# A two-layer decoder trunk on one core: weight parts of large expert slots taken earlier, a third tile loaded ahead of a loop, small steps of a norm on ScalarE

## The chip, the cores and the metric

One NeuronCore of a Trainium2 chip runs the whole program. Time is device microseconds (us) of one execution; a comparison takes the median of several. Lower is better.

## What is computed

Two layers over 1024 tokens of width 1024, in float32. Layer 0 mixes tokens with a gated DeltaNet beside an S5 state-space model, layer 1 with dilated sliding-window attention. After each mixer comes a hierarchical mixture of experts, and after both a post-norm residual:

```
h = layer_norm(alpha * h + mixer(h))
# per token: best of 4 groups, best 2 of its 8 experts; 32 experts in all
y = gate1 * expert1(h) + gate2 * expert2(h)
expert(x) = (silu(x @ w_gate) * (x @ w_up)) @ w_down      # 1024 -> 512 -> 1024
h = layer_norm(alpha * h + y)       # rsqrt(var + 1e-5), scale, shift
```

The weights of the experts are 6 MB each, 192 MB a layer, and all of them are read in each layer.

## The kernel before

**Slots.** In each layer `moe` runs 32 slots, one an expert. Experts are sorted by how many tokens chose them: the first 16 slots are large (up to 128 tokens), the last 16 are small (up to 64 tokens). The order is three large slots, then rounds of two small and two large ones (S S L L), and at the end S S L S S with large slot 15 between small ones. A round is 24 weight tiles.

**Weights.** An expert's weights come in six tiles of 1 MB (`raw_weights`, L457), all through SP's queue into 17 buffers. Tiles 0 to 3 hold gate and up, tiles 4 and 5 hold down. Load number n waits until load n-3 has landed, so that three are under way; the issue of a load thus marks the landing of the one three before it. A small slot multiplies the raw tile in plain float32 (`small`, L589 and L605). A large slot uses split products: `weights` cuts each tile into halves, ScalarE makes a rounded copy `whi` of each half (L488), VectorE makes the rest `wlo` = raw - `whi` (L490), and TensorE adds three products, hi-hi, lo-hi and hi-lo (L529, L530 for gate and up, L547 for down). The pairs `whi`, `wlo` are the "parts"; there are five buffers for parts, each of one half.

**Order within `moe`.** Each slot is a generator in four pieces: gather and transposition of its rows; halves k = 0 to 3 (tiles 0, 1); halves k = 4 to 7 (tiles 2, 3), the activation `hdn`, its transposition `ph` and split `hh`, `hl`; the down product `po` or `pos` (tiles 4, 5), its copy `ot` or `ots` out of PSUM and a scatter by POOL to `yd`. In program order the first piece of the next slot comes before the third of this one, and the next slot's second piece before this one's fourth. So between halves k = 3 and k = 4 of a large slot that follows a small one stands the small one's down product with its copy `ots` (L618); `ots` is put behind the last `whi` that was traced. Between `hh` of a large slot and its down product stand halves k = 0 to 3 of the next. The order of each engine's instructions is fixed when the program is built, from the program's order and modelled durations.

**The last two slots.** Slots S7 and S15 write no rows to `yd`; their outputs stay in SBUF (`held`), and `combine` adds them by a product with a selection matrix (`hot`). S15 takes all its loads in one go; the last five loads of a layer wait for buffers.

**After the slots.** `tail` and `head` load the first tiles (128 tokens each) of `combine` behind the last weight load: `HEADS` says how many, 1 in layer 0 and 2 in layer 1, with the residual row `ca` and the two expert rows `cyh`. For these VectorE adds the gated rows (L820, L822). Then comes a loop for overflowing experts, which runs no time here (384 weight loads, two times 192), with a point where all engines and the loads under way meet (L747). `scatter_held` then writes the held rows to `yd`, and the other tiles' rows `cy` are read behind it.

**`combine` in layer 1.** Tiles 0 to 3 are summed on TensorE: the residual times the identity or alpha (`al`, L861), plus for t >= 2 two gated rows (`cdg`, L867), plus for t < 2 the held rows (L864). ScalarE copies the sum out with its total (L870), VectorE makes the mean (L881). For tiles 4 to 7 VectorE adds alpha times the residual itself (L872). Then ScalarE squares (L882) while VectorE does (a - mean) * g (L883). `end` of the tile before follows: variance plus eps on VectorE (L887), root on ScalarE (L212), a reciprocal with one Newton step on VectorE (L213 to L216), and the last product and sum (L889). The order on VectorE and ScalarE is by hand: norm(t), then end(t-1). Layer 0's `combine` is alike, with the sums on VectorE and the next layer's value projection (L1078) on TensorE between.

Of the kernel before, what the change touches and what calls it, by code (L numbers as in the profile page):

```python
# [10 lines left out]
F32 = mybir.dt.float32  # L11
# [3 lines left out]
AF = mybir.ActivationFunctionType  # L15
OP = mybir.AluOpType
# [3 lines left out]
D = 1024  # L20
S = 1024
NT = 8
KT = 8
NE = 32
ALPHA = 4.0 ** 0.25
LN_EPS = 1e-5
# [7 lines left out]
LARGE = 16  # L34
# [2 lines left out]
BLOCKS = 24  # L37

PAUSE = (12, 13)

HEADS = (1, 2)

# [115 lines left out]
class Trunk:  # L158
# [48 lines left out]

    def rsqrt(self, v, w):

        nc = self.nc  # L210
        s, r, q, n, o = (w[:, i:i + 1] for i in range(5))
        nc.scalar.activation(s, v, AF.Sqrt)  # L212
        nc.vector.reciprocal(r, s)  # L213
        nc.vector.scalar_tensor_tensor(q, r, v, r, op0=OP.mult, op1=OP.mult)  # L214
        nc.vector.tensor_scalar(n, q, -0.5, 1.5, op0=OP.mult, op1=OP.add)  # L215
        nc.vector.tensor_mul(o, r, n)  # L216
# [288 lines left out]
                                     self.ident)  # L505
        return px.rearrange("p (k t) -> p k t", k=4)

    def large(self, hd, yd, xg, gi, si, wsrc, wk, ps):


        nc = self.nc
        self.hold.setdefault("g", self.gather(hd, xg, gi))
        xh = wk.tile([128, KT, 128], F32R, name="xh", tag="xh")
        xl = wk.tile([128, KT, 128], F32R, name="xl", tag="xl")
        for a in range(2):
            s = self.split(self.transposed(xg, a, ps), xh[:, 4 * a:4 * a + 4], xl[:, 4 * a:4 * a + 4])
            self.hold.setdefault("x", s)
        yield
        pg = ps.tile([128, 512], F32, name="pg", tag="pg")
        pu = ps.tile([128, 512], F32, name="pu", tag="pu")  # L520
        for k in range(KT):
            if k == KT // 2:
                yield
            if k % 2 == 0:
                W = self.weights(wsrc(k // 2))
            hi, lo = W[k % 2]
            for i, (x, w) in enumerate(((xh, hi), (xh, lo), (xl, hi))):
                s, z = k == 0 and i == 0, k == KT - 1 and i == 2
                nc.tensor.matmul(pg, x[:, k], w[:, 0:512], start=s, stop=z)  # L529
                nc.tensor.matmul(pu, x[:, k], w[:, 512:1024], start=s, stop=z)  # L530
        hdn = wk.tile([128, 512], F32, name="hdn", tag="hdn", bufs=1)
        nc.scalar.activation(hdn, pg, AF.Silu)  # L532
        nc.vector.tensor_mul(hdn, pu, hdn)
        ph = ps.tile([128, 512], F32, name="ph", tag="m")
        for f in range(4):
            nc.tensor.transpose(ph[:, f * 128:(f + 1) * 128], hdn[:, f * 128:(f + 1) * 128], self.ident)
        hh = wk.tile([128, 4, 128], F32R, name="hh", tag="hh", bufs=1)
        hl = wk.tile([128, 4, 128], F32R, name="hl", tag="hl", bufs=1)
        self.split(ph.rearrange("p (k t) -> p k t", k=4), hh, hl)
        yield  # L540
        W = [w for q in (4, 5) for w in self.weights(wsrc(q))]
        po = [ps.tile([128, 512], F32, name=f"po{a}", tag="po") for a in range(2)]
        for f in range(4):
            hi, lo = W[f]
            for i, (x, w) in enumerate(((hh, hi), (hh, lo), (hl, hi))):
                for a in range(2):
                    nc.tensor.matmul(po[a], x[:, f], w[:, a * 512:(a + 1) * 512],  # L547
                                     start=(f == 0 and i == 0), stop=(f == 3 and i == 2))
        ot = wk.tile([128, D], F32, name="ot", tag="ot", bufs=1)
        nc.scalar.activation(ot[:, 0:512], po[0], AF.Copy)  # L550
        nc.vector.tensor_copy(ot[:, 512:1024], po[1])
        yield nc.gpsimd.indirect_dma_start(  # L552
            out=yd, out_offset=bass.IndirectOffsetOnAxis(ap=si, axis=0),
            in_=ot, in_offset=None, bounds_check=2 * S - 1, oob_is_err=False)
# [68 lines left out]
    def moe(self, l, hd, yd, first, small, order, place, ov, over, gate, hp, xp, wk, ps, tail):  # L623

        nc, tc = self.nc, self.tc
# [3 lines left out]
        xg = xp.tile([128, D], F32, name="xg")  # L629
# [3 lines left out]
        def enter(s):  # L633
            if s < FIXED:
                def src(q):
                    return wm[l, s, q]
            else:
                reg = []

                def src(q):  # L640
                    if not reg:
                        reg.append(nc.sync.value_load(order[0:1, s:s + 1], min_val=0, max_val=NE - 1))
                    return wmv[ds(reg[0] * 6 + q, 1)].rearrange("a p n -> p (a n)")
            if s < LARGE:
                return self.large(hd, yd, xg, first[:, 1, s:s + 1], first[:, 0, s:s + 1], src, wk, ps)
            j = s - LARGE
            g = SMALL + j % (SMALL // 2)
            return self.small(hd, yd, xg, small[:, g:g + 1], small[:, j:j + 1], src, X,
                              {SMALL // 2 - 1: 0, SMALL - 1: 1}.get(j), wk, ps)


        seq, larges = [*range(FIXED)], list(range(FIXED, LARGE))
        for j in range(SMALL // 2):
            seq += [LARGE + j, LARGE + j + SMALL // 2] + larges[2 * j:2 * j + 2]
        scat = []
        self.ends = [(None, None), None]
        run = enter(seq[0])
# [4 lines left out]
        for i in range(NE):  # L662
# [6 lines left out]
            st = next(run)  # L669
# [154 lines left out]
    def combine(self, l, hd, yd, gate, rows, hot, diag, wk, ps, nx, done):  # L824
# [2 lines left out]

        nc = self.nc
        E = self.held["E"]
        H = len(hot)  # L830
        halves = [slice(c * 512, (c + 1) * 512) for c in range(2)]
        g, b = (wk.tile([128, D], F32, name=n, bufs=1) for n in ("fg", "fb"))
        first = self.bcast_rows(g, self.I["lnfg"][l], D)
        self.bcast_rows(b, self.I["lnfb"][l], D)
        Y, A, ST = {}, dict(enumerate(rows)), {}

        def load(t):
            Y[t] = wk.tile([128, 2, D], F32, name="cy", tag="cy", bufs=NT if l else 3)
            if t >= H:
                A[t] = wk.tile([128, D], F32, name="ca", tag="ca", bufs=NT - H if l else 2)  # L840
                r = self.row_tile(t, hd, A[t], False)
                if l and t > H + 1:
                    self.behind(r, self.loaded)
                self.loaded = self.y_tile(t, yd, Y[t])

# [7 lines left out]
        def norm(t):  # L853
            a, st, y = A[t], ST[t], Y[t]
            if l:
                al, dg = diag
                pe = t < 4
                p = ps.tile([128, D], F32, name="cp", tag="cp", bufs=4)
                for h in halves:
                    if pe:  # L860
                        nc.tensor.matmul(p[:, h], self.ident if t < H else al, a[:, h], start=True, stop=False)  # L861
                for i, h in enumerate(halves):
                    if t < H:
                        nc.tensor.matmul(p[:, h], hot[t][i], E[i], start=False, stop=True)  # L864
                    else:
                        for k in range(2):
                            nc.tensor.matmul(p[:, h], dg[:, t - H, k], y[:, k, h],  # L867
                                             start=(k == 0 and not pe), stop=(k == 1))
                if pe:
                    nc.scalar.activation(a, p, AF.Copy, accum_out=st[:, 0:1])  # L870
                else:
# [1 line left out]
            elif t < H:  # L873
# [4 lines left out]
                    nc.vector.scalar_tensor_tensor(a[:, h], p, 1.0, a[:, h], op0=OP.mult, op1=OP.add,  # L878
                                                   accum_out=st[:, o:o + 1])
                nc.vector.tensor_tensor(st[:, 0:1], st[:, 0:1], st[:, 9:10], op=OP.add)  # L880
            nc.vector.tensor_scalar(st[:, 1:2], st[:, 0:1], -1.0 / D, None, op0=OP.mult)  # L881
            nc.scalar.activation(y[:, 0], a, AF.Square, bias=st[:, 1:2], accum_out=st[:, 2:3])  # L882
            nc.vector.scalar_tensor_tensor(y[:, 1], a, st[:, 1:2], g, op0=OP.add, op1=OP.mult)  # L883

        def end(t):
            a, st, y = A[t], ST[t], Y[t]
            nc.vector.tensor_scalar(st[:, 3:4], st[:, 2:3], 1.0 / D, LN_EPS, op0=OP.mult, op1=OP.add)  # L887
            self.rsqrt(st[:, 3:4], st[:, 4:9])
            nc.vector.scalar_tensor_tensor(a, y[:, 1], st[:, 8:9], b, op0=OP.mult, op1=OP.add)  # L889

        with self.tc.manual_schedule(engines={mybir.EngineType.DVE, mybir.EngineType.Activation}):
# [1194 lines left out]
    def run(self):  # L2086
        nc, I = self.nc, self.I
        with self.pool("c") as p:
# [19 lines left out]
            for l in range(2):  # L2108
# [25 lines left out]
                with self.pool(f"mx{l}", side="right") as xp, self.pool(f"rawb{l}", RAWB, side="right") as rawb, \  # L2134
# [7 lines left out]
                    nx = {}  # L2142

                    def head():
                        for t in range(H):
                            self.row_tile(t, hd, nx["rows"][t], True)
                            self.y_tile(t, yd, nx["ys"][t])
                            e = self.gated(t, nx["rows"][t], nx["ys"][t], gate)
                        return e

                    def tail():
# [9 lines left out]
                            op = hp  # L2161
                        else:
                            vp = op = nx["vp"] = alloc("cr")
                            nx["ys"] = [vp.tile([128, 2, D], F32, name=f"cyh{t}") for t in range(H)]
                            al = vp.tile([128, 128], F32, name="al")
                            nc.vector.tensor_scalar(al, self.ident, ALPHA, None, op0=OP.mult)
                            dg = vp.tile([128, NT - H, 2, 128], F32, name="cdg")
                            for u in range(H, NT):
                                for k in range(2):
                                    nc.vector.tensor_scalar(dg[:, u - H, k], self.ident, gate[:, u, k:k + 1], None,  # L2170
                                                            op0=OP.mult)
                            nx["diag"] = al, dg
                        nx["rows"] = [vp.tile([128, D], F32, name=f"ca{t}") for t in range(H)]
                        nx["hot"] = [self.held_rows(t, [op.tile([128, 128], F32, name=f"hot{l}{t}{e}")
                                                        for e in range(2)]) for t in range(H)]
                        with self.tc.issue_after(self.flight[-1]):
                            if l == 0:
                                self.value_loads(nx["V"], range(1), None)
# [97 lines left out]
```

## Time and profile before

| what | value |
|---|---|
| median of 3 runs | 2457.79 us (2455.66 to 2460.64) |
| the profiled execution's own time | 2459.88 us |
| its span in the profile | 2458.1 us |
| TensorE busy | 92% of the span |
| VectorE, ScalarE busy | 60%, 46% |
| DMA moved | 561.5 MB, mean 228 GB/s |
| mean granted TensorE clock | 0.969 |

PE is TensorE's matmuls, PEld its weight loads, DVE VectorE, ACT ScalarE, POOL GpSimd, SP the engine that issues loads. A wait in the profile is idle time of an engine, put down to what ended it. The expert stages run from about 650 to 1200 us and from 1860 to 2403 us; in what follows a place is one slot's wait.

### The profile page before, as it was taken

What the parts mean: (1) busy time and instruction counts of PE and PEld (TensorE: products, weight loads), DVE (VectorE), ACT (ScalarE), POOL (GpSimd) and SP (SyncE); (2) the same over time, 40 slices, a digit from 0 to 9 for tenths busy, and PEclk for the clock granted to TensorE, in tenths of its full rate; (3) what the DMA queues carried; (4) which work ended last, traced back from release to release, by engine and by line L of the source; (5) the groups of instructions that cost most, each with busy time, mean ns of one, the idle gap of its engine ahead of it and who ended that gap; (6) DMA issues with size and microseconds to landing.
All of it is one profiled execution on the core that took longest, in us unless ns stands there. A gap on an engine that the chain in (4) does not pass through costs nothing. (4 is left out here: it accounts for less than half of the span.)

```text
span 2458.1 us, 34057 instructions
## 1 busy us (share of the span) xinstructions
PE 2258.3 (92%) x11948; PEld 1625.6 (66%) x11948; DVE 1484.9 (60%) x3025; ACT 1141.1 (46%) x1871; POOL 443.9 (18%) x548
## 2 busy tenths in 40 slices
PE   7999999889699999999699999998997999999986
PEld 5888899778555555554377888887875555555542
DVE  7565646557864555554473777778578545555536
ACT  5435454442453544443333666667225534444423
POOL 1545434100114111100001111113001321111100
PEclk9999999899899999999899999999998999999998
DMA  4222222354599999997741000012837999999977
GB/s 166 61 66 42 66 63 72 109 215 158 198 403 373 412 407 410 401 401 309 290 156 49 33 29 33 29 39 85 297 110 288 363 411 405 406 407 406 400 302 269
DMA packets 181728, 561.50 MB, mean 228 GB/s; under 512 B 61570, under 2 KB 98818, under 8 KB 131888
## 3 DMA queue, kind: packets, MB, share of 16 engines
q1 hardware_dynamic: 166000, 525.03, 56.5%
q0 software_dynamic: 15552, 34.25, 3.6%
q8 instruction: 96, 1.57, 0.3%
q14 instruction: 80, 0.66, 0.1%
HBM read 518.76 MB, written 56.43 MB: 234 GB/s over the span
## 5 line engine op out<-in xcount | busy, mean ns | idle before, releaser
L490 DVE TENSOR_TENSOR wlo<-wraw,whi 128x1024 fp32r<-128x1024 f32 x384 | 451.1, 1219 | 144.3 <-ACT whi L488 124.6
L488 ACT ACTIVATE whi<-wraw 128x1024 fp32r<-128x1024 f32 x384 | 383.5, 1053 | 71.9 <-PE pu L530 49.5
L589 PE MATMUL pgs<-wraw,xs 128*64 128x512 f32 x1024 | 241.2, 602 | 1.3 <-ACT hdn L532 0.9
L589 PEld LDWEIGHTS pgs<-wraw,xs 128*64 128x64 f32 x1024 | 68.4, 137 | 129.0 <-issue 117.7
L173 PE MATMUL pj<-xTh,phi 128*128 128x512 f32 x320 | 131.5, 415 | 13.2 <-ACT xTh L446 13.2
L529 PE MATMUL pg<-whi,xh 128*128 128x512 f32 x256 | 108.1, 422 | 28.4 <-ACT whi L488 22.8
L173 PE MATMUL pj<-xTh,plo 128*128 128x512 f32 x320 | 132.2, 414 | 0.0
L173 PE MATMUL pj<-xTl,phi 128*128 128x512 f32 x320 | 130.7, 409 | 0.0
L605 PE MATMUL pos<-wraw,hs 128*64 128x512 f32 x512 | 121.4, 609 | 5.5 <-ACT hdns L592 3.3
L1217 POOL TENSOR_TENSOR plo<-praw,phi 128x256 fp32r<-128x256 f32 x64 | 53.0, 830 | 400.6 <-ACT phi L1216 397.6
L529 PE MATMUL pg<-wlo,xh 128*128 128x512 f32 x256 | 110.7, 432 | 11.3 <-DVE wlo L490 10.7
L173 PE MATMUL opo<-ohi,oyp 128*128 128x512 f32 x392 | 115.0, 401 | 2.0 <-DVE oyp L447 2.0
L1233 PE MATMUL pj<-xTh,phi 128*128 128x512 f32 x256 | 114.8, 449 | 1.9 <-DVE KL L1249 1.0
L1118 ACT ACTIVATE sm<-sm,st 128x1024 f32<-128x1024 f32 (+7 forms) x128 | 99.2, 776 | 35.8 <-DVE st L1117 34.3
L1114 DVE CUSTOM_DVE_ANT_0 sm<-s,amask 128x1024 f32<-128x1024 f32 (+7 forms) x128 | 96.5, 755 | 20.7 <-PE s L1110 18.9
L552 POOL DMA_INDIRECT yd<-ot,first x32 | 40.2, 1255 | 364.0 <-issue 177.0
L529 PE MATMUL pg<-whi,xl 128*128 128x512 f32 x256 | 103.5, 404 | 0.7 <-DVE xl L447 0.7
L1131 PE MATMUL pp<-cf,sm 128*128 128x128 f32 x576 | 95.0, 276 | 9.8 <-ACT yt L1156 4.3
L530 PE MATMUL pu<-whi,xh 128*128 128x512 f32 x256 | 103.2, 403 | 0.0
L530 PE MATMUL pu<-whi,xl 128*128 128x512 f32 x256 | 102.8, 402 | 0.0
L530 PE MATMUL pu<-wlo,xh 128*128 128x512 f32 x256 | 102.7, 401 | 0.0
L1233 PE MATMUL pj<-xTl,phi 128*128 128x512 f32 x256 | 101.4, 396 | 0.0
(564 smaller groups left out, 5151.8 us busy)
## 6 DMA issues: line engine op xcount, KB each, us to landing
wraw<-in_wm SPq DMA_DIRECT2D x384, 1024.0 KB
cy<-yd SPq DMA_DIRECT2D x26, 512.0 KB
praw<-in_win SPq DMA_DIRECT2D x40, 256.0 KB
oraw<-in_wo SPq DMA_DIRECT2D x16, 512.0 KB
hd<-or SPq DMA_DIRECT2D x16, 512.0 KB
ca<-hd SPq DMA_DIRECT2D x16, 512.0 KB
praw<-in_wqk SPq DMA_DIRECT2D x64, 128.0 KB
oy<-ytd SPq DMA_DIRECT2D x14, 448.0 KB
```

Of the source, the lines that this page charges most:

```text
L173: self.last = self.nc.tensor.matmul(*args, **kw).ins
L488: self.last_hi = nc.scalar.activation(hi, r[:, h], AF.Copy)
L490: nc.vector.tensor_tensor(lo, r[:, h], hi.bitcast(F32), op=OP.subtract)
L529: nc.tensor.matmul(pg, x[:, k], w[:, 0:512], start=s, stop=z)
L530: nc.tensor.matmul(pu, x[:, k], w[:, 512:1024], start=s, stop=z)
L589: nc.tensor.matmul(pg[r].rearrange("p (g f) -> p g f", g=2), x[:, k], w[:, k % 2, a], start=(k == 0), stop=(k == KT - 1))
L605: nc.tensor.matmul(po[r], hs[:, f % 2, f // 2], W[f // 2][:, o:o + 512], start=(f == 0), stop=(f == 3))
L1114: nc.vector.tensor_tensor_reduce(out=sm[:, :n], in0=s[:, :n], in1=am[:, 1024 - n:1024], scale=1.0, scalar=-3e38, op0=OP.add, op1=OP.max, a ...
L1118: nc.scalar.activation(sm[:, :n], sm[:, :n], AF.Exp, bias=st[:, 1:2], accum_out=st[:, 2:3])
L1131: nc.tensor.transpose(pp[:, (j - j0) * 128:(j - j0 + 1) * 128], sm[:, j * 128:(j + 1) * 128], self.ident)
L1217: nc.gpsimd.tensor_tensor(lo, r, hi.bitcast(F32), op=OP.subtract)
L1233: nc.tensor.matmul(p, w[:, o], x[:, k, cs], start=(k == 0 and i == 0), stop=(k == KT - 1 and i == 2))
```

## The change

Four things are changed.

1. A large slot is told whether the slot before it and the slot after it are small (`near`). If the one before is small, its third tile (halves k = 4, 5) is loaded and split at the end of its second piece, so before the small slot's down tiles and `ots`; this is so at seven slots of a layer (3, 5, ... 15). If the one after is small, its fifth tile (the first of down) is loaded and split before `hh` and `hl`, and `hh` is put behind its last `whi`; this is so at eight slots (2, 4, ... 14 and 15).
2. In layer 1 `head` loads the rows of a third tile too (t = 2), without gating them; `combine` adds the held rows to it by `hot`, as it was read before `scatter_held`.
3. `PEH` = 5: tile 4 of layer 1 is summed on TensorE and copied by ScalarE like tiles 0 to 3.
4. The mean of tiles 0 to 4 of layer 1 is made by ScalarE. In both layers the root is taken by ScalarE straight from the sum of squares with eps as a bias, and a second ScalarE instruction makes variance plus eps for the Newton step; VectorE's L887 goes.

```diff
+PEH = 5
...
     def rsqrt(self, v, w):
+        self.nc.scalar.activation(w[:, 0:1], v, AF.Sqrt)
+        self.newton(v, w)
+
+    def newton(self, v, w):
...
-        nc.scalar.activation(s, v, AF.Sqrt)
...
-    def large(self, hd, yd, xg, gi, si, wsrc, wk, ps):
+    def large(self, hd, yd, xg, gi, si, wsrc, wk, ps, before=False, behind=False):
...
+        W = []
         for k in range(KT):
             if k == KT // 2:
+                if before:
+                    W += self.weights(wsrc(2))
                 yield
-            if k % 2 == 0:
-                W = self.weights(wsrc(k // 2))
-            hi, lo = W[k % 2]
+            if len(W) <= k:
+                W += self.weights(wsrc(k // 2))
+            hi, lo = W[k]
...
-        self.split(ph.rearrange("p (k t) -> p k t", k=4), hh, hl)
+        W = self.weights(wsrc(4)) if behind else []
+        with self.tc.issue_after(self.last_hi.ins) if behind else nullcontext():
+            self.split(ph.rearrange("p (k t) -> p k t", k=4), hh, hl)
         yield
-        W = [w for q in (4, 5) for w in self.weights(wsrc(q))]
+        for q in (4, 5)[len(W) // 2:]:
+            W += self.weights(wsrc(q))
...
+        near = {s: tuple(0 <= j < NE and seq[j] >= LARGE for j in (i - 1, i + 1)) for i, s in enumerate(seq)}
...
     def combine(...):
-        H = len(hot)
+        H = HEADS[l]
...
+        eps = wk.tile([128, 1], F32, name="eps", bufs=1)
+        nc.vector.memset(eps, LN_EPS)
...
+        if l:
+            Y[H] = nx["ys"][H]
...
         def norm(t):
-                pe = t < 4
+                pe = t < PEH
...
-                    if t < H:
-                        nc.tensor.matmul(p[:, h], hot[t][i], E[i], start=False, stop=True)
-                    else:
+                    if t >= H:
                         for k in range(2):
                             nc.tensor.matmul(p[:, h], dg[:, t - H, k], y[:, k, h],
-                                             start=(k == 0 and not pe), stop=(k == 1))
+                                             start=(k == 0 and not pe), stop=(k == 1 and t >= len(hot)))
+                    if t < len(hot):
+                        nc.tensor.matmul(p[:, h], hot[t][i], E[i], start=False, stop=True)
...
-            nc.vector.tensor_scalar(st[:, 1:2], st[:, 0:1], -1.0 / D, None, op0=OP.mult)
+            if l and t < PEH:
+                nc.scalar.activation(st[:, 1:2], st[:, 0:1], AF.Copy, scale=-1.0 / D)
+            else:
+                nc.vector.tensor_scalar(st[:, 1:2], st[:, 0:1], -1.0 / D, None, op0=OP.mult)
...
         def end(t):
-            nc.vector.tensor_scalar(st[:, 3:4], st[:, 2:3], 1.0 / D, LN_EPS, op0=OP.mult, op1=OP.add)
-            self.rsqrt(st[:, 3:4], st[:, 4:9])
+            nc.scalar.activation(st[:, 4:5], st[:, 2:3], AF.Sqrt, bias=eps, scale=1.0 / D)
+            nc.scalar.activation(st[:, 3:4], st[:, 2:3], AF.Identity, bias=eps, scale=1.0 / D)
+            self.newton(st[:, 3:4], st[:, 4:9])
...
                     def head():
-                        for t in range(H):
-                            self.row_tile(t, hd, nx["rows"][t], True)
+                        for t in range(H + l):
+                            self.row_tile(t, hd, nx["rows"][t], t < H)
                             self.y_tile(t, yd, nx["ys"][t])
-                            e = self.gated(t, nx["rows"][t], nx["ys"][t], gate)
+                            if t < H:
+                                e = self.gated(t, nx["rows"][t], nx["ys"][t], gate)
```

The tiles that these need (`ys`, `rows`, `hot`) are allocated for `H + l` tiles in the same places.

## Rows read from the trace of the kernel before

**Rows 1.** One round of each layer: length; busy PE, PEld, DVE, ACT, POOL; clock, DMA share, GB/s.

```profile
1008.00:1076.40 68.40, 62.23 (x279) 36.27 (x277) 36.73 (x40) 30.94 (x40) 8.10 (x7) 1.00 1.01 403
2142.80:2210.50 67.70, 63.60 (x280) 37.56 (x278) 36.72 (x40) 31.03 (x41) 8.10 (x7) 0.97 1.00 408
```

**Rows 2.** Waits of the load queue over the run: us, times, longest.

```profile
SPq L457 <- DMA wraw<-in_wm: 767.1, 334, 7.0
```

**Rows 3.** TensorE waits, layer 0, 800 to 1175 us.

```profile
PE pg L529 <- ACT whi L488: 10.4, 6, 2.0
PE po L547 <- ACT whi L488: 8.2, 5, 1.6
...
PE pg L529 <- DVE wlo L490: 4.8, 10, 0.5
PE po L547 <- DVE wlo L490: 3.0, 6, 0.5
```

**Rows 4.** TensorE waits, layer 1, 1995 to 2375 us.

```profile
PE pg L529 <- ACT whi L488: 10.1, 6, 1.7
PE pg L529 <- DVE wlo L490: 5.9, 11, 1.2
```

**Rows 5.** Timeline, ScalarE and TensorE, at a large slot's third tile: start, us.

```profile
2153.65 0.60 ACT L618 ACTIVATE ots<-pos 128x512 f32<-128x512 f32 x1 [7.93 <-PE pos L605]
2154.14 1.99 ACT L488 ACTIVATE whi<-wraw 128x1024 fp32r<-128x1024 f32 x2
...
2155.24 0.50 PE L529 MATMUL pg<-whi,xh 128*128 128x512 f32 x1 [1.69 <-ACT whi L488]
...
2156.50 0.50 PE L529 MATMUL pg<-wlo,xh 128*128 128x512 f32 x1 [0.52 <-DVE wlo L490]
```

**Rows 6.** Timeline at a large slot's fifth tile, layer 0.

```profile
1049.90 0.60 ACT L446 ACTIVATE hh<-ph 128x512 fp32r<-128x512 f32 x1 [2.08 <-PE ph L536]
...
1051.47 4.63 DVE L490 TENSOR_TENSOR wlo<-wraw,whi 128x1024 fp32r<-128x1024 f32 x4 [0.25 <-ACT whi L488]
...
1051.49 0.73 PE L547 MATMUL po<-whi,hh 128*128 128x512 f32 x2 [1.63 <-ACT whi L488]
...
1052.75 0.73 PE L547 MATMUL po<-wlo,hh 128*128 128x512 f32 x2 [0.52 <-DVE wlo L490]
```

**Rows 7.** Stretches of lower granted clock in the stages with expert weights, columns as in 1.

```profile
883.80:887.20 3.40, 3.40 (x8) 2.72 (x9) 3.40 (x4) 3.39 (x4) 0.00 (x0) 0.50 0.95 361
...
2358.40:2361.80 3.40, 3.40 (x9) 2.62 (x9) 2.61 (x3) 0.78 (x1) 0.00 (x0) 0.50 1.02 423
```

**Rows 8.** Timeline: load issues of both layers, and ScalarE's first copies of slot 15.

```profile
1049.21 0.33 SPq L457 DMA_DIRECT2D wraw<-in_wm  x1
...
1115.86 0.33 SPq L457 DMA_DIRECT2D wraw<-in_wm  x1
...
1142.51 2.00 ACT L488 ACTIVATE whi<-wraw 128x1024 fp32r<-128x1024 f32 x2
...
2326.39 0.33 SPq L457 DMA_DIRECT2D wraw<-in_wm  x1
...
2342.69 2.00 ACT L488 ACTIVATE whi<-wraw 128x1024 fp32r<-128x1024 f32 x2
```

**Rows 9.** Timeline of TensorE in the last `combine`.

```profile
2405.06 2.75 PE L861 MATMUL cp<-ca,cf 128*128 128x512 f32 x4 [2.54 <-DVEq L747]
...
2418.21 7.53 PE L867 MATMUL cp<-cy,cdg 128*128 128x512 f32 x16 [0.88 <-DMA cy<-yd]
```

**Rows 10.** Timeline of VectorE in the last `combine`.

```profile
2436.51 1.22 DVE L872 SCALAR_TENSOR_TENSOR ca<-ca,cp 128x1024 f32<-128x1024 f32 x1
...
2437.96 1.28 DVE L883 SCALAR_TENSOR_TENSOR cy<-ca,fst,fg 128x1024 f32<-128x1024 f32 x1
...
2441.62 1.22 DVE L872 SCALAR_TENSOR_TENSOR ca<-ca,cp 128x1024 f32<-128x1024 f32 x1
```

**Rows 11.** Four us before the last `combine`, columns as in 1.

```profile
2401.00:2405.00 4.00, 1.52 (x8) 0.29 (x4) 3.50 (x4) 0.67 (x2) 0.00 (x0) 1.00 0.02 6
```

More of the change, by code (lines that the diff above doesn't have):

```diff
@@ L644, in enter @@
             if s < LARGE:
-                return self.large(hd, yd, xg, first[:, 1, s:s + 1], first[:, 0, s:s + 1], src, wk, ps)
+                return self.large(hd, yd, xg, first[:, 1, s:s + 1], first[:, 0, s:s + 1], src, wk, ps, *near[s])
             j = s - LARGE
@@ L835, in combine @@
         Y, A, ST = {}, dict(enumerate(rows)), {}
+        if l:
+            Y[H] = nx["ys"][H]
         def load(t):
-            Y[t] = wk.tile([128, 2, D], F32, name="cy", tag="cy", bufs=NT if l else 3)
-            if t >= H:
-                A[t] = wk.tile([128, D], F32, name="ca", tag="ca", bufs=NT - H if l else 2)
+            if t not in Y:
+                Y[t] = wk.tile([128, 2, D], F32, name="cy", tag="cy", bufs=NT - 1 if l else 3)
+            if t >= len(rows):
+                A[t] = wk.tile([128, D], F32, name="ca", tag="ca", bufs=NT - len(rows) if l else 2)
                 r = self.row_tile(t, hd, A[t], False)
-                if l and t > H + 1:
+                if l and t > len(rows) + 1:
                     self.behind(r, self.loaded)
@@ L2163, in tail @@
                             vp = op = nx["vp"] = alloc("cr")
-                            nx["ys"] = [vp.tile([128, 2, D], F32, name=f"cyh{t}") for t in range(H)]
+                            nx["ys"] = [vp.tile([128, 2, D], F32, name=f"cyh{t}") for t in range(H + l)]
                             al = vp.tile([128, 128], F32, name="al")
@@ L2172, in tail @@
                             nx["diag"] = al, dg
-                        nx["rows"] = [vp.tile([128, D], F32, name=f"ca{t}") for t in range(H)]
+                        nx["rows"] = [vp.tile([128, D], F32, name=f"ca{t}") for t in range(H + l)]
                         nx["hot"] = [self.held_rows(t, [op.tile([128, 128], F32, name=f"hot{l}{t}{e}")
-                                                        for e in range(2)]) for t in range(H)]
+                                                        for e in range(2)]) for t in range(H + l)]
                         with self.tc.issue_after(self.flight[-1]):
```

## Prediction

> **What bounds the kernel now.** I read first the page's table of slices, which shows two long stages with the DMA engines full; these are the expert stages, and most of the change lies in them. Then the stretches of one round (S S L L, 24 weight tiles): TensorE is busy for 62.2 of 68.4 us in layer 0 and 63.6 of 67.7 us in layer 1, and the DMA engines' share is 1.00 in both [rows 1]. Both look like the bound, so the next question is which one waits for the other. SP's waits say that a weight load waits nearly always for a load before it (767.1 us, at 334 of 384 loads) [rows 2]: the stream of weights runs at its own rate. TensorE's list of waits holds none for a weight tile in either layer; the largest are for parts, `whi` and `wlo` [rows 3, 4]. So TensorE runs behind the stream, and the distance is what a faster TensorE can win. It is read at large slot 15, the last one: its first tile is load 172 of the layer, whose landing load 175 marks, and ScalarE's first copy of it comes at 1142.51 against 1115.86 for that load in layer 0 (26.7 us) and at 2342.69 against 2326.39 in layer 1 (16.3 us) [rows 8]. The tiles lie there for that long. In layer 0 load 151, a round earlier, went out at 1049.20 [rows 8]: the stream's round is 66.7 us, less than TensorE's 68.4, so there the distance grows. At the end of a layer the last five loads wait for buffers that TensorE's work frees, so the end of the stage follows TensorE, not the stream.
>
> **Third tile ahead.** At the third tile of a large slot after a small one ScalarE sits idle for 7.93 us, because the next instruction in its queue is `ots`, which waits for the small slot's last product; only then does it copy the third tile's halves. TensorE, done with that product, waits 1.69 us for `whi` and 0.52 us for `wlo` [rows 5]. The change puts these two copies ahead of `ots`, into the idle time: 2.0 us of ScalarE and two `wlo` on VectorE. Nothing behind them is late: `ots` waits for TensorE longer than they take. The place is paid six times in layer 0 (10.4 us for `whi`, of the 4.8 for `wlo` 6 x 0.52 = 3.1) [rows 3], together 13.5 (rounded), and six times in layer 1 (10.1 + 3.1 = 13.2) [rows 4]; the seventh place, at slot 3, shows no such wait. I take both sums whole. Below, the bound is half, if the built order still leaves one half behind `ots`; above, nothing more.
>
> **Fifth tile ahead.** In layer 0, at five of the eight places, `hh` comes first on ScalarE and the fifth tile's copies behind it; TensorE waits 1.63 and 0.52 us [rows 6], in sum 8.2 + 3.0 = 11.2 [rows 3]. ScalarE idles 2.08 us ahead of `hh` [rows 6], and two copies take 1.99 us [rows 5], so they just fit. Then TensorE can start when `hh` is done, 1049.90 + 0.60 = 1050.50 instead of 1051.49: 0.94 to 1.0 us won. The wait for `wlo` goes too, but `hl` now stands behind two `wlo` on VectorE, of which four take 4.63 [rows 6], and can give up to 0.5 us back. I take 1.2 a place, in sum 6; bounds 2 and 11. Layer 1 has no row of L547 for `whi`; of its 5.9 us for `wlo` [rows 4] 2.8 are not the third tile's. I take 1 for the fifth tile; bounds -2 (`hh` stands behind two copies now) and 3.
>
> **The clock.** Behind six of these waits the granted clock is 0.50, the 1.2 GHz level, for 3.4 us each, two in layer 0 and four in layer 1; the first and the last are shown [rows 7]. Each costs half of that, 1.7 us. Not each wait was followed by one, and other short waits remain, so I take half: 1.7 us in layer 0 and 3.4 in layer 1; bounds nothing and all (3.4 and 6.8).
>
> **What the distance allows.** Layer 0 would win 13.5 + 6 + 1.7 = 21.2 us, less than the 26.7 of [rows 8]. Layer 1 would win 13.2 + 1 + 3.4 = 17.6, of which five sixths, about 14.7, come before slot 15, where 16.3 are there. Gather and scatter move ahead with TensorE and take some of the stream: a round moves 408 GB/s x 67.7 us = 27.6 MB [rows 1], of it 24 x 1.05 = 25.2 weights, so 15 us ahead brings 0.5 MB forward, 1.3 us. That leaves 15.0, just enough; for the scrape I count 17. The swapped loads cost less than that: the small slot's last two tiles land one load later, 66.7 / 24 = 2.8 us.
>
> The stream itself runs at 403 and 408 GB/s [rows 1]. The Trainium skill (DMA: Bandwidth & Descriptors, Where 436 GB/s comes from) puts the limit of loads from HBM at about 358 GB/s a core and that of the SBUF ports at 435. By the first a round would need 27.6 / 0.358 = 77 us, TensorE would wait for tiles and this change would be worth nothing; the trace disagrees, with its 408 GB/s. By the second, an estimate from that page, a round cannot be under 63.4 us.
>
> **Third tile of the last `combine`, and five tiles on TensorE.** TensorE starts at 2405.06, after the meeting of engines. It then runs without a pause but for 0.88 us ahead of tile 2's `cdg` products at 2418.21, where it waits for the rows; sixteen of these, for tiles 2 and 3, take 7.53 us, so a set of four takes 1.88 [rows 9]. The early load can win those 0.88 us and no more, and it adds a set of `hot` to tile 2 and, by `PEH`, a set of `al` to tile 4. So tiles 2 and 3 are summed at 2418.21 - 0.88 + 7.53 + 1.88 = 2426.7, tile 4 at 2426.7 + 1.88 + 3.77 = 2432.4. ScalarE's copy and the mean come next; a pass over 1024 columns takes 1.28 on VectorE [rows 10], and I take 1.7 for both. VectorE's step from one L872 to the next is 2441.62 - 2436.51 = 5.11, of it 1.45 up to L883 [rows 10]; the rest, 3.66, is what tile 4 still costs it. Tile 5 starts at 2432.4 + 1.7 + 3.66 = 2437.8 instead of 2436.51, 1.3 us late, and the steps after it stay as they were but for one small instruction less a tile. Also the meeting of engines waits for the loads under way: the DMA engines are idle (0.02) from 2401 on [rows 11]; 1.5 MB more, at 400 GB/s 3.9 us, ends at about 2405, and the start slips by 0.4. With a little back for the smaller steps this part costs +1.5; bounds -1.5 (if the sums of tile 4 are no bound) and +3.
>
> **Root and mean.** ScalarE's new instructions take the place of VectorE's one for one. All small instructions and hops of a step of VectorE are 5.11 - 1.22 - 2 x 1.28 = 1.3 us [rows 10]; I count nothing for the exchange, with 0.2 us a tile either way, 1.6 for the eight tiles of layer 1, inside the bounds of the last part. In layer 0 the value projection's products stand between the tiles; without that cover it would be as much again.
>
> **Sum.** 2459.9 (the profiled execution's own time) - 21.2 - 17 + 1.5 = 2423.2. It stands 2.1 us above the median of the runs and within their range; I say 2424 and leave the rest to waits that only show when others are gone.
>
> **Rivals.** (1) *The stream is the bound after all* (2438 to 2452): the distance cannot be used, because TensorE's new waits for landing tiles bring the lower clock, or because the last loads of a layer wait as long as before. For it speaks the DMA share of 1.00 [rows 1]; against it that no wait for a tile shows anywhere. What remains is the excess of TensorE's round over the stream's, 68.4 - 66.7 = 1.7 us in layer 0 over five rounds, and the last slot's own two waits in each layer (2.2 and 2.15 in layer 0, 2.2 in layer 1): about 15, and +1.5, so 2446. (2) *The parts don't come earlier* (2458 to 2462): the order on ScalarE is built from modelled durations; if the model has the third tile landing late, the copies stay behind `ots`. Against it: the load itself now stands ahead of the small slot's tiles. It would leave +1.5. (3) *Slower: TensorE loses its filler* (over 2463). In layer 1 half a small slot's products stand between `ph` and the down product and hide `hh`; so it has no such wait as the 2.15 us of layer 0 [rows 6]. The order is built anew; where such products no longer stand in a gap, the place costs up to 2.15 us, and 3.0 with half a stretch of the lower clock. Some 30 places in both layers have such filler. It decides from 37 / 3.0 = 12 lost places on; at 18 it would cost 54, net +18, so 2478. For it speaks that layer 0 has lost it at five places already; against it that the change moves loads towards where the work is.
>
> **How the numbers follow.** Forecast 0.70, rival 1 0.16, rival 2 0.05, rival 3 0.09. The forecast's own range: layer 0 between -12 and -26, layer 1 between -9 and -19, the tail between -1.5 and +3, not all at one end: 2410 to 2438. With rival 1 the range reaches to 2447. A measurement of this kernel tells 0.2%, 4.9 us, from no change. Faster: 0.70 + 0.16 = 0.86; same: 0.05; slower: 0.09.
>
> **What the profile after would show.** Right: TensorE's waits for `whi` at L529 fall from 10 us in a layer to under 2, those at L547 in layer 0 from 8 to under 3; the idle time before `ots` on ScalarE shrinks by 2 us a place; layer 0's stage ends some 21 us earlier, layer 1's takes 17 less; at slot 15 of layer 1 the distance is near nothing, and in layer 0 some 6 us. The last `combine` has VectorE waiting at tiles 3 and 4. Wrong: waits of TensorE for `wraw`, a lower clock in other places, or the third tile's copies still behind `ots`.

## The result, and the profile after

The changed kernel takes 2441.76 us (median of 5 runs, 2433.54 to 2446.71) against 2457.79: a ratio of 0.9931, 95% interval 0.9909 to 0.9953. It is faster, by 16 us; the forecast was 36 us less than the profiled execution of before. The profiled executions (2443.14 and 2459.88 us) differ by 16.7 us as well, so the traces can be set side by side. Stage by stage: up to the first expert product of layer 0, -5.9 us; layer 0's expert stage 534.0 us instead of 550.7, -16.7; between the stages +1.3; layer 1's stage 548.8 instead of 543.9, **+4.9**; from its end to the end of the span 55.2 instead of 55.6, -0.4. The two stages, first before, then after, in the columns of [rows 1]:

```profile
648.40:1199.10 550.70, 503.30 (x2216) 296.81 (x2215) 300.01 (x373) 248.96 (x309) 83.51 (x73) 0.99 0.96 378
1858.60:2402.50 543.90, 506.07 (x2216) 298.69 (x2215) 302.20 (x387) 249.16 (x308) 83.91 (x73) 0.98 0.97 384
...
642.50:1176.50 534.00, 500.82 (x2216) 296.67 (x2215) 299.61 (x373) 249.72 (x309) 80.71 (x73) 0.99 0.99 390
1837.30:2386.10 548.80, 508.49 (x2216) 301.37 (x2215) 303.01 (x389) 249.66 (x308) 84.25 (x73) 0.97 0.97 382
```

The first -5.9 is in code that the change doesn't touch: 2.4 us add up in small differences along the mixer, and the first gather lands 3.4 us earlier (TensorE waits 6.6 us for it, before 10.0). In the traces of the other runs, where that code is the same, layer 0's stage starts at 641.8 to 647.5 us, so this part is one execution against another.

So the forecast of -21.2 for layer 0 is near in size, though not by its terms, and that of -17 for layer 1 is wrong in sign. One round of each layer, in the columns of [rows 1]:

```profile
992.80:1058.50 65.70, 61.97 (x280) 36.35 (x277) 36.46 (x40) 30.94 (x41) 7.69 (x7) 1.00 1.00 398
2125.10:2191.60 66.50, 61.47 (x279) 36.48 (x278) 36.45 (x40) 30.95 (x40) 8.56 (x7) 1.00 1.00 404
```

These two rounds have no stretch of lower clock; others have. The five rounds from slot 5 to slot 15 take 333.1 us (before 342.8) in layer 0 and 338.5 (before 337.4) in layer 1. TensorE's waits in the stages, to be held against [rows 3, 4]; first layer 0, 780 to 1155 us, then layer 1, 1975 to 2360 us (us, times, longest):

```profile
PE pg L538 <- ACT whi L493: 9.9, 6, 1.7
PE pg L538 <- DVE wlo L495: 5.9, 11, 1.2
...
PE pg L538 <- ACT whi L493: 9.9, 6, 1.7
PE pg L538 <- DVE wlo L495: 5.9, 11, 1.2
...
PE ph L545 <- DVE hdn L542: 3.5, 3, 1.2
```

The gate and up products wait as long for their parts as before, in both layers. The rows of the down product in layer 0, 8.2 and 3.0 us in [rows 3], are gone. Where the first wait now stands, the timeline of ScalarE and TensorE shows at large slot 9 of layer 1, the slot of [rows 5]:

```profile
2128.87 2.00 ACT L493 ACTIVATE whi<-wraw 128x1024 fp32r<-128x1024 f32 x2
2138.87 0.60 ACT L630 ACTIVATE ots<-pos 128x512 f32<-128x512 f32 x1 [8.00 <-PE pos L617]
2139.36 3.89 ACT L493 ACTIVATE whi<-wraw 128x1024 fp32r<-128x1024 f32 x4
...
2131.91 0.40 PE L538 MATMUL pg<-whi,xh 128*128 128x512 f32 x1
...
2136.88 1.94 PE L617 MATMUL pos<-wraw,hs 128*64 128x512 f32 x8
2140.46 0.50 PE L538 MATMUL pg<-whi,xh 128*128 128x512 f32 x1 [1.64 <-ACT whi L493]
...
2141.72 0.50 PE L538 MATMUL pg<-wlo,xh 128*128 128x512 f32 x1 [0.53 <-DVE wlo L495]
```

The third tile's copies come early indeed (2128.87). But TensorE uses them at once: its products of halves k = 4 and 5 (from 2131.91) now run *before* the small slot's down product `pos` is done. Its end moves back by as much, and with it `ots`; ScalarE is idle for 8.00 us ahead of `ots`, before 7.93. Behind `ots` now stands the fourth tile's first copy, and TensorE waits 1.64 and 0.53 us for it at half k = 6, where it had waited 1.69 and 0.52 at k = 4. The wait has moved by one tile.

At the fifth tile of slot 12 in layer 0, the slot of [rows 6]:

```profile
1024.55 3.90 ACT L493 ACTIVATE whi<-wraw 128x1024 fp32r<-128x1024 f32 x4
1029.95 0.60 ACT L541 ACTIVATE hdn<-pg 128x512 f32<-128x512 f32 x1 [1.50 <-PE pg L538]
1032.63 0.60 ACT L451 ACTIVATE hh<-ph 128x512 fp32r<-128x512 f32 x1 [2.09 <-PE ph L545]
...
1031.94 0.66 PE L545 MATMUL ph<-cf,hdn 128*128 128x128 f32 x4
1032.53 1.94 PE L601 MATMUL pgs<-wraw,xs 128*64 128x512 f32 x8
1034.39 0.73 PE L559 MATMUL po<-whi,hh 128*128 128x512 f32 x2
```

The fifth tile's copies are made with the fourth's, even before `hdn`, and eight products of the next small slot stand between `ph` and the down product, where none stood before. The down product waits for nothing.

The last norm, TensorE, ScalarE and VectorE:

```profile
2388.86 2.78 PE L879 MATMUL cp<-ca,cf 128*128 128x512 f32 x4 [2.74 <-SPq L760]
...
2407.83 17.33 PE L883 MATMUL cp<-cy,cdg 128*128 128x512 f32 x40
...
2414.89 1.02 ACT L888 ACTIVATE ca<-cp 128x1024 f32<-128x1024 f32 x1 [0.44 <-PE cp L883]
...
2419.95 1.22 DVE L890 SCALAR_TENSOR_TENSOR ca<-ca,cp 128x1024 f32<-128x1024 f32 x1
```

No wait for rows is left on TensorE. The meeting of the engines ends on the loads now, 2.74 us of idle time where [rows 9] show the start behind 2.54, and tile 5 starts on VectorE 31.1 us after TensorE's start (before 2436.51 - 2405.06 = 31.5, by [rows 9, 10]).

### The profile page after: what moved, and what is told of

The parts are those of the page before. It is cut to its first block, busy times and chain, and to the rows that moved or that the text cites. A ratio compares the mean times of both kernels' runs of the same rounds, so it can differ in the third digit from the quotient of the medians.

```text
span 2441.3 us, 34100 instructions
## 1 busy us (share of the span) xinstructions
PE 2254.0 (92%) x11956; PEld 1627.3 (67%) x11956; DVE 1480.5 (61%) x3006; ACT 1147.6 (47%) x1894; POOL 437.7 (18%) x548
## 5 line engine op out<-in xcount | busy, mean ns | idle before, releaser
L175 PE MATMUL pj<-xTh,phi 128*128 128x512 f32 x320 | 131.5, 415 | 13.2 <-ACT xTh L451 13.2
L175 PE MATMUL pj<-xTh,plo 128*128 128x512 f32 x320 | 132.1, 413 | 0.0
L538 PE MATMUL pg<-wlo,xh 128*128 128x512 f32 x256 | 110.4, 431 | 13.0 <-DVE wlo L495 12.5
L1255 PE MATMUL pj<-xTh,plo 128*128 128x512 f32 x256 | 101.4, 396 | 0.2
```

Of the source, the lines that this page charges most:

```text
L175: self.last = self.nc.tensor.matmul(*args, **kw).ins
L1255: nc.tensor.matmul(p, w[:, o], x[:, k, cs], start=(k == 0 and i == 0), stop=(k == KT - 1 and i == 2))
```

## The experiments

Two theories at first. **M**: the third tile's wait only moved, that part wins nothing, and the fifth tile in layer 0 carries the gain. **T**: the third tile wins as forecast, and something else in layer 1 eats it. The parts were taken singly first. All times below are compared with the kernel before, run beside each kernel on the same chip (its medians there were 2460.8 to 2466.1 us), so the ratio is what counts; "us" differences are the ratio times 2458.

**Fifth tile without the third, third without the fifth, neither.**

```diff
-                return self.large(..., src, wk, ps, *near[s])
+                return self.large(..., src, wk, ps, False, near[s][1])   # fifth only
+                return self.large(..., src, wk, ps, near[s][0], False)   # third only
+                return self.large(..., src, wk, ps)                      # neither
```

> The changed kernel without the third tile ahead: large slots split only the fifth tile early; tail, root and mean as changed. Theory M (the third tile's wait only moved to the fourth tile, so that part wins nothing; the fifth tile in layer 0 carries the gain): 2439 to 2447 us, within 4 us of the changed kernel, and TensorE's waits for `whi` of about 10 us a layer stand at half k = 4 again. Rival T (the third tile's parts do win, half of the 13 us a layer, and something else in layer 1 eats it): 2450 us or more, still below the kernel before by 3 to 8 us.

> The changed kernel without the fifth tile ahead: large slots split only the third tile early; tail, root and mean as changed. Theory M: 2454 to 2459 us, no more than 4 us from the kernel before; waits for `whi` of about 10 us a layer at half k = 6, and those of the down product in layer 0 (8 and 3 us) still there. Rival T: 2440 to 2450 us.

> Neither tile ahead; only the third tile's early load for the last norm, five tiles summed on TensorE, and root and mean on ScalarE. By the sum of the prediction +1.5 us (2459); by the changed kernel's trace, in which the end of the last slot to the end of the span is 55.2 us against 55.6, -0.4 (2457). Both lie inside what a time can tell here, so the trace decides: from the meeting of the engines to the start of tile 5 on VectorE 31.1 us (the trace's way) against 32.8 (the sum's way; 31.5 before).

Measured: fifth only 2441.53 us, ratio 0.9916 (0.9895 to 0.9936); third only 2477.04 us, 1.0057 (1.0036 to 1.0079); neither 2474.39 us, 1.0051 (1.0032 to 1.0070). Taking the third tile ahead changes nothing that can be told, with the fifth (0.9931 against 0.9916) or without it (1.0057 against 1.0051): T falls. But neither theory had the last number. The tail's parts alone cost 12.5 us, and the fifth tile wins 33 us on top of them, not the 11 of [rows 3]. TensorE's waits in the two expert stages fall from 94 to 72 us between these two traces; the rest of the 33 is not accounted for. The tail itself is not slower: from TensorE's start behind the meeting to tile 5 it takes 31.1 us (2447.55 - 2416.46), the trace's way, and from the end of the last slot to the end of the span 55.2 us, as in the changed kernel. The loss is in layer 1's expert stage, 556.5 us where the kernel before takes 543.9; layer 0's takes 550.8, as before. Both stages with the tail's parts alone:

```profile
646.00:1196.80 550.80, 502.84 (x2216) 296.48 (x2215) 300.60 (x373) 249.80 (x309) 82.79 (x73) 0.99 0.95 378
1857.20:2413.70 556.50, 507.71 (x2216) 297.95 (x2215) 303.94 (x389) 249.09 (x308) 82.72 (x73) 0.98 0.95 377
```

From slot 5's first product to slot 15's it is 343.9 us in layer 1, before 337.4. So a new theory, **O**: one of the tail's parts changes the order that is built for layer 1's expert stage, and that order loses what [rows 4] show, a down product that needn't wait. In the order of TensorE's instructions that the traces show, layer 1's stage with the tail's parts is the same, product for product, as layer 0's; in the kernel before they differ. With root and mean left on VectorE both stages keep the order of before.

**The tail without root and mean, and root and mean alone.**

```diff
-            nc.scalar.activation(st[:, 4:5], st[:, 2:3], AF.Sqrt, bias=eps, scale=1.0 / D)
-            nc.scalar.activation(st[:, 3:4], st[:, 2:3], AF.Identity, bias=eps, scale=1.0 / D)
-            self.newton(st[:, 3:4], st[:, 4:9])
+            nc.vector.tensor_scalar(st[:, 3:4], st[:, 2:3], 1.0 / D, LN_EPS, op0=OP.mult, op1=OP.add)
+            self.rsqrt(st[:, 3:4], st[:, 4:9])
```

(and the mean by VectorE; the other run has these lines as changed, with `H` tiles loaded ahead and `PEH = 4`)

> Neither tile ahead, root and mean on VectorE as before: only the third tile's early load and the fifth tile on TensorE in the last norm. The order of TensorE's instructions in both expert stages is that of the kernel before. Theory O (moving root and mean changes what the builder thinks of the times, and so the order of layer 1's expert stage, which loses products between `ph` and the down product; that is the 12 us by which the run with the tail alone was slower): within 5 us of the kernel before, more likely 1 us below than above. Rival L (the early loads or the fifth tile's sums cost it): 8 to 13 us above the kernel before.

> The kernel before with nothing but root and mean on ScalarE. Theory O: the order of TensorE in layer 1's expert stage becomes that of layer 0, TensorE's waits of the down product for `whi` show in layer 1 too (four or five of 2.2 us and the clock stretches behind them), and the time is 9 to 14 us above the kernel before. Rival L: within 5 us of it.

Measured: without root and mean 2465.82 us, ratio 1.0017 (1.0005 to 1.0028), +4 us; root and mean alone 2472.98 us, 1.0049 (1.0029 to 1.0069), +12 us. O holds. The +4 is small but clear of noise, and on the side that was thought the less likely; in its trace 2.7 us of it lie behind the last slot (58.3 us to the end of the span, before 55.6). TensorE's waits in layer 1 of the second run (1995 to 2385 us) have the two rows that layer 0 has in [rows 3]:

```profile
PE pg L538 <- ACT whi L493: 10.1, 6, 1.7
PE po L559 <- ACT whi L493: 8.2, 5, 1.6
...
PE po L559 <- DVE wlo L495: 3.0, 6, 0.5
```

Layer 1's stage takes 554.4 us in this trace, before 543.9, and its order is again that of layer 0. So an edit of instructions of 0.2 us in a norm cost some 12 us in another stage, by another order of TensorE there; orders are built from modelled times, and which time tipped this one is not known. Layer 0's stage takes 555.2 us here (before 550.7) in an unchanged order: the granted clock is 0.50, the 1.2 GHz level, for 24.5 us of it, before 13.6. A few us between two traces can be that.

**The third tile with TensorE's old order.** If M is right, the cure is to keep halves k = 4 and 5 behind `pos`, so that they cover `ots` and the copy behind it.

```diff
+                with self.tc.issue_after(self.last_pos.ins) if before and k == KT // 2 else nullcontext():
                     nc.tensor.matmul(pg, x[:, k], w[:, 0:512], start=s, stop=z)
                     nc.tensor.matmul(pu, x[:, k], w[:, 512:1024], start=s, stop=z)
```

(`last_pos` is the small slot's last down product)

> The changed kernel, and TensorE's products of the third tile's halves are put behind the small slot's down product, where they stood before. Then that product, and with it `ots`, is early, and halves k = 4 and 5 (2.9 us) cover `ots` and the fourth tile's first copy (0.6 + 1.05 us). Theory M: waits of TensorE for `whi` and `wlo` fall from 16 us a layer to under 3, and the lower clock behind them goes; layer 0 wins 10 to 13 us more (12.5 us of distance to the stream are left at its last large slot), layer 1 13 to 18: 2411 to 2422 us. Rival S (the stream of weights is the bound, the distance can't be used): 2432 to 2442 us with TensorE waiting for tiles. Rival N (the wait moves to the next place again): 2436 to 2446 us with 10 us a layer at another tile.

Measured: 2416.49 us, ratio 0.9826 (0.9802 to 0.9850): 26 us less than the changed kernel (0.9931), as M has it. In the traces layer 0's stage takes 523.3 us (-10.7 against the changed kernel) and layer 1's 524.0 (-24.8, more than expected), and the end of the span comes 6.0 us later behind the last slot. Over both stages TensorE waits 53.9 us, in the changed kernel 71.5, and its granted clock is 0.50 for 25 us, in the changed kernel 47. TensorE's waits in layer 1, 1975 to 2363 us, then the last round of each layer in the columns of [rows 1], then ScalarE at slot 15 of layer 1:

```profile
PE cp L881 <- SPq L762: 8.1, 1, 8.1
PE phs L609 <- DVE hdns L606: 8.0, 6, 3.3
PE ph L546 <- DVE hdn L543: 3.5, 3, 1.2
PE pg L539 <- DVE wlo L495: 2.6, 5, 1.2
```

```profile
1052.50:1114.80 62.30, 60.77 (x280) 37.04 (x278) 36.49 (x40) 32.19 (x40) 8.00 (x7) 1.00 1.00 402
2237.70:2300.80 63.10, 61.95 (x287) 37.80 (x286) 36.26 (x41) 31.08 (x40) 8.05 (x7) 1.00 1.00 399
```

```profile
2299.37 2.01 ACT L493 ACTIVATE whi<-wraw 128x1024 fp32r<-128x1024 f32 x2 [0.41 <-DMA wraw<-in_wm]
...
2302.35 2.01 ACT L493 ACTIVATE whi<-wraw 128x1024 fp32r<-128x1024 f32 x2 [0.49 <-DMA wraw<-in_wm]
2304.83 2.01 ACT L493 ACTIVATE whi<-wraw 128x1024 fp32r<-128x1024 f32 x2 [0.47 <-DMA wraw<-in_wm]
```

The wait for `whi` is gone and `wlo` is down to 2.6. Now ScalarE waits for the tile to land, and copies it as it lands: the distance of [rows 8] is used up by the last large slot, and the meeting of the engines waits 8.1 us for the loads under way. At the last large slot the stream is the bound, in layer 0 as well: ScalarE's waits for tiles there sum to 3.6 us in layer 0 and 3.9 in layer 1, where the changed kernel has none. The prediction had put the end of the distance at about this gain.

**Both tiles ahead instead.**

```diff
-                    W += self.weights(wsrc(2))
+                    W += self.weights(wsrc(2)) + self.weights(wsrc(3))
```

> The changed kernel, with third and fourth tile loaded and split ahead of the small slot's down product (instead of holding TensorE's products back). Theory M: no copy stands behind `ots` any more, so the waits of 10 and 6 us a layer go as in the run with the products held back, and the stream of weights becomes the bound: 2411 to 2424 us. Rival N (four copies don't fit into ScalarE's 7.9 us with the fifth tile's and `hh`, or the five part buffers hold them back, and the wait stands at `hdn` or `hh`): 2428 to 2445 us.

Measured: 2467.71 us, ratio 1.0031 (1.0014 to 1.0049), slower than before and outside both expectations. TensorE's waits in layer 0, 795 to 1160 us, then TensorE and ScalarE at one place:

```profile
PE pg L538 <- ACT whi L493: 12.0, 9, 1.5
PE pg L538 <- DVE wlo L495: 9.4, 15, 1.4
...
PE po L559 <- ACT hh L451: 2.7, 4, 0.7
```

```profile
954.39 0.60 ACT L630 ACTIVATE ots<-pos 128x512 f32<-128x512 f32 x1 [1.28 <-PE pos L617]
...
955.36 2.95 ACT L493 ACTIVATE whi<-wraw 128x1024 fp32r<-128x1024 f32 x3
...
956.47 0.50 PE L538 MATMUL pg<-whi,xh 128*128 128x512 f32 x1 [1.54 <-ACT whi L493]
...
957.73 0.50 PE L538 MATMUL pg<-wlo,xh 128*128 128x512 f32 x1 [0.52 <-DVE wlo L495]
```

TensorE takes all four halves of the third and fourth tile before `pos`; `ots` comes later still, and behind it stand `hh` and the copies of the *next* large slot's first tile. The wait moved once more, and there are now nine places instead of six. It is rival N, and worse than N was priced. What counts is not which copies are put past `ots`, but how early `pos` is.

**The third tile with the old order, without the fifth.** The edit is that of the run with the products held back, with `near[s][0], False`.

> Third tile ahead with TensorE's products held behind the small slot's down product, without the fifth tile ahead; tail, root and mean as changed. Its like without the third tile is the run with the tail alone (2474 us, 12 above the kernel before). Theory M (the third tile's sums of 13.5 and 13.2 us are there to be won if TensorE's order is kept): 25 to 36 us below that run, the 36 with the clock stretches, so 2438 to 2449 us, and the waits for `whi` of gate and up fall under 2 us a layer. Rival W (another wait takes their place, as with both tiles ahead): 2455 us or more.

Measured: 2431.01 us, ratio 0.9868 (0.9846 to 0.9889), 45 us below the run with neither tile: more than expected. TensorE's waits in layer 1, 1995 to 2375 us, say why:

```profile
PE pg L539 <- ACT whi L493: 2.4, 2, 1.2
PE po L560 <- DVE wlo L495: 1.8, 5, 0.4
PE pg L539 <- DVE wlo L495: 1.4, 4, 0.4
```

The order that is built now has a filler ahead of the down product too, so its 8.2 us went with the third tile's, though nothing was done for the fifth tile. The two parts of the change overlap.

**What of the tail is worth anything once the stream is the bound.** Three runs on the run with the products held back: without the early third tile's rows; with root and mean on VectorE; with the whole tail of before (`H` tiles ahead, `PEH = 4`, root and mean on VectorE).

> The run with the third tile's products held back, without the early load of the third tile's rows in the last norm (two tiles ahead as before; five on TensorE as changed). With the stream as the bound the meeting of the engines waits for the loads under way, 8.1 us in layer 1; 1.5 MB less at 400 GB/s would end 3.7 us sooner, and tile 2 then waits about 0.9 us or more for its rows: 1 to 3 us faster (2413 to 2416 us). Rival: the wait only moves behind the meeting, to tile 2's rows: 2416 to 2419 us.

> Third and fifth tile ahead with the products held back, root and mean on VectorE as before. With the stream of weights as the bound of both expert stages the order of TensorE there matters little, and the tail costs what the steps of the last norm say: up to 3 us above the run with the products held back (58.2 us from the end of the last slot to the end of the span in the tail-only run without root, 55.3 with it): 2416 to 2420 us. If root and mean change the expert stage here too, 2421 us or more.

> Only the expert slots changed: third and fifth tile ahead with the products held back; last norm, root and mean as in the kernel before. If the tail's parts are worth nothing beside a stage bound by the stream, the same time as with them, 2413 to 2420 us; if the early third tile and root on ScalarE win what the step times say (0.4 to 1 us), no run can tell it; if the early loads cost at the meeting of the engines, where 8.1 us were waited, 2410 to 2414.

Measured: 2417.41 us, ratio 0.9829 (0.9808 to 0.9850); 2419.28 us, 0.9819 (0.9798 to 0.9840); 2420.04 us, 0.9817 (0.9797 to 0.9838). None can be told from the run with the products held back (0.9826). Without the early rows the meeting's wait falls from 8.1 to 6.0 us and 0.5 us come back at tile 2: the direction expected, but too little for a time to tell. The fastest kernel of the study is any of these four, at about 0.982.

## Why the prediction was right in sign and half in size

*The range, and layer 0.* That the range holds 2441.76 us is luck. The forecast's own range ended at 2438; it was widened to 2447 for rival 1, the stream as the bound, and rival 1 is not what happened: neither TensorE nor ScalarE waits for a weight tile in the changed kernel's expert stages. Layer 0's -16.7 beside a forecast of -21.2 is luck too: the 13.5 of the third tile came to nothing, the fifth tile gave 11.2 instead of 6, and 3.1 us come before slot 5, where TensorE's largest single wait was 3.5 us before and is 2.5 now.

*Third tile ahead, -13.5 and -13.2: the step that failed.* "Nothing behind them is late" took TensorE's order as given. With its parts ready, the built order put halves k = 4 and 5 ahead of `pos`, `ots` came later by what these products take, and the same wait stood at k = 6. The measured worth is nothing that can be told in either setting (+3.7 and +1.5 us, inside the intervals). "Half" as the lower bound was wrong too; I had looked for copies left behind `ots`, which is rival 2, and not for the next tile's copy coming to stand there. The sums themselves were there to be won: with TensorE's order kept, the waits fell from 15.8 us to 2.6 in layer 1. The Trainium skill (PSUM — Partial Sum Buffer, Engine vs sequencer instructions) says that ScalarE's queue is strictly first in, first out. The rows agree: at 2138.87 ScalarE starts `ots` after 8.00 idle us, and the fourth tile's copy only behind it, at 2139.36.

*Fifth tile, -6 and -1: mis-sized.* In layer 0 all 11.2 us of [rows 3] went, not 6: the copies were done before `hdn`, not merely before `hh`, and a filler came back between `ph` and the down product. In layer 1 the term rested on a wrong reading: the 2.8 us were taken from the row of the gate and up products in [rows 4], which the fifth tile doesn't serve. The down product's own waits there, 1995 to 2375 us before, were these:

```profile
PE po L547 <- ACT hh L446: 1.6, 3, 0.7
PE po L547 <- DVE wlo L490: 1.4, 4, 0.4
```

The term of -1 also hid that the other edits would have cost 12 there; the fifth tile ahead won that back too.

*Root and mean, 0: the other step that failed.* Their own cost in the norm is as small as said (54.9 us from the last slot's end to the end of the span with them alone, 55.6 before; beside the tail's other parts one trace each has 55.3 with them and 58.3 without). But they changed the order of another stage: rival 3, the lost filler, at the places where it was priced (2.15 us each), by a cause that I had not thought of. At +12 it didn't reach the point where it decides, and the fifth tile undid it.

*Layer 1's +4.9.* Of this 4.1 us come before slot 5: TensorE waits 4.2 us for a gather of a small slot (before 2.4) that stands on POOL behind sixteen writes of a table, while all its waits there grow by only 1.5 us, from 8.1 to 9.6. The rest is the clock: it is 0.50 for 9.9 us there, before 4.8, and over the whole stage for 33.8 us, before 25.3, which at half speed costs 4.2 us more; its waits grow by 2.8 in all, from 36.7 to 39.5, and the two together are 2 us more than the +4.9. In the rounds the waits for `hdn` are new (3.5 us above) and those for `hh` (0.5) and `wlo` of the down product shrink. How much of this is the change and how much one execution was not separated; the five executions of the changed kernel run from 2433.54 us at a mean granted clock of 0.973 to 2446.71 at 0.968, and the run with the fifth tile only, of about the same time, has 540.2 us in layer 1's stage and 541.7 in layer 0's.

*Clock, -1.7 and -3.4.* Nothing came in layer 0 (13.4 us at 0.50, before 13.6), and layer 1 lost 4.2, as just said. The waits for `whi` and `wlo` of the gate and up products are still there. With these gone, in the run with the products held back, the clock did come back: 10.6 us at 0.50 in layer 0 and 14.3 in layer 1.

*Last norm, +1.5.* Measured -0.4. TensorE's products were over-counted: the sixteen that took 7.53 us before were carried over as they stood, and forty of L883 now take 17.33 us, so sixteen take 6.9, and TensorE is done with tile 4 26.0 us after its start, not 27.3. The meeting did come to wait for the loads, as said.

*The distance.* By the reading of [rows 8] it is 1123.78 - 1111.07 = 12.7 us in layer 0 after the change (before 26.7) and 23.4 in layer 1 (before 16.3): the first used by half, the second grown. That it can be used whole the run with the products held back shows; rival 1 falls as the bound of this change, and becomes the bound at 2416 us.

## What to carry to other kernels

A copy that waits for a late product holds up all that is behind it in its queue; putting one copy past it moves the stall to the next, unless the product itself comes sooner, so ask what the *consumer* does with the early data and whether it delays the product that the stall hangs on. Where orders are built from modelled times, compare the built orders of every stage before and after an edit, however far from the stage it is: 0.2 us instructions in a norm cost 12 us in a stage of expert products here. And take the parts of a combined change singly: this one is +12.5, -33 and 0, and the part that is worth nothing is worth 26 us once one order is held.

## What was unexpected of the hardware

With TensorE faster or slower, the DMA engines moved 404 to 406 GB/s over the five rounds of a layer, in both layers and in all of these kernels, though these rounds took from 318 to 348 us; a round's length fell to 62.3 and 63.1 us in the last rounds of the run with the products held back, while its loads had been landing ahead. That is under the 63.4 us that the prediction gives as the least for a round: its figure is of the loads of a round, and these went on at 402 and 399 GB/s. A profile that shows both TensorE and the DMA engines full can have room for 45 us.
